# A streaming Conformer layer on one core: the second block's first attention head gets the longer lag between its q and k request and its scores

## The chip, the cores and the metric

The kernel runs on one core of a Trainium2 chip. The metric is the device time of one execution in microseconds, as the median of several runs. A core has a matrix engine (TensorE, in the profile PE, its weight loads PEld), a vector engine (VectorE, DVE), a scalar engine (ScalarE, ACT), GpSimd (POOL) and SyncE (SP), whose queue issues most DMAs. Each engine works through its own instructions in order.

## The reference

One layer works on 2048 prompt rows and 64 sample rows of width 1024. A normalised and modulated input goes through one projection whose columns are a convolution pair, q, k, v and two gates; a causal depthwise convolution and a banded attention run on it, are gated, merged and projected; a feed-forward part follows.

```python
h = rms_norm(x, p['norm1_g']) * (1 + sc1) + sh1
z = h @ p['w_in']
glu_a, glu_b, q, k, v, g_conv, g_attn = jnp.split(z, offs, axis=-1)
u = glu_a * jax.nn.sigmoid(glu_b)
conv_out, conv_state = conv_module(u, conv_hist, ...)
q = rms_norm(q.reshape(B, T, N_HEADS, HEAD_DIM), p['q_norm_g'])
k = rms_norm(k.reshape(B, T, N_HEADS, HEAD_DIM), p['k_norm_g'])
o = attend(q, k, v, p['rel_bias']).reshape(B, T, ATTN_DIM)
attn_out = o @ p['w_attn_out']
merged = jax.nn.sigmoid(g_conv) * conv_out + jax.nn.sigmoid(g_attn) * attn_out
x = x + gt1 * (merged @ p['w_o'])
...
s = jnp.einsum('bqhd,bkhd->bhqk', q, k).astype(jnp.float32) * ATTN_SCALE
s = s + rel_bias[:, rel].astype(jnp.float32)[None]
p = jax.nn.softmax(jnp.where(mask[None, None], s, NEG_INF), axis=-1)
return jnp.einsum('bhqk,bkhd->bqhd', p, v)
```

There are 8 heads of 64 columns. Each frame reads its own chunk of 64 frames and the eight chunks before.

## The kernel before

All products in float32 are made of three matmuls on parts: `hh` and `hl` are the high and low part of the normalised input, `whi` and `wlo` those of a weight, and `mm3` issues hh·whi, hh·wlo and hl·whi into one accumulator `ps`. Three such matmuls are called a triple here.

The prompt and the sample are cut into four blocks of tokens (`PBLOCKS`; block 0 holds the 64 sample rows and 512 prompt rows, blocks 1 to 3 hold 512 each). `ORDER` runs for each block q, the first convolution stage, k, the second, v, the third and fourth, and the gates. In eight of the convolution stages of blocks 1 and 2 a step of the modulation is put in (`mod_steps`): products of `cl` with four slabs `wmod` of 512 KB into `pa`, and some microseconds later a short product with `sel` (`pa<-sel,R`). Four slabs are held; a slab's next load goes out when its products are done.

The attention of a block starts after its v (`heads`, `HEADS_NS`) and runs between the projection products of the stages that follow. It isn't written out in place. Each head is a generator (`attend`) in a lane, and a lane is pumped each time the emitted matmuls add up to `STEP_NS` of modelled PE time. The clock of all this is `stream.load["pe"]`, the planner's sum of modelled PE time in nanoseconds: a generator yields the time from which it may go on. PE's instructions stay in the order in which they were emitted (`manual_schedule` for PE); those of the other engines and of the DMA queues are ordered by a scheduler.

A head of block 1, 2 or 3 does this:

- `fetch` (L1491) requests q and k (`load_qk`, tiles `q2` and `kk`, one buffer each) and the bias, and sets in `loaded[i]` the planner time from which the scores may be emitted: `lag` after the request, `QK_LAG` = 9000 ns or `FIRST_LAG` = 14000 ns, and no less than `BIAS_LAG` = 6000 ns. For all but the first head of a block it is called when the last scores of the head before are emitted.
- four tiles of 128 queries: four matmuls `sc<-kk,q` of 320 columns each into `sc` (one buffer), then on DVE the row maximum with the bias added (`pr,sm<-sc,bias`, in the orders below an `ISA` row), the exponential on ACT, and the scaling on ACT.
- five groups of transposes (`ptp<-ident,pr`), the split into `ph` (ACT) and `pl` (DVE), and the products with v (`po<-ph,vv` and `po<-pl,vv`).

DVE also works through the 31 taps of the convolution (`y<-u,wd,y`), which the scheduler places around the row maxima; a tap is not to be issued ahead of the latest maximum emitted before it (`ahead_of_taps`).

`order` is the list of all heads as (block, head). In block 0 the prompt's heads (0, h) and the sample's ("s", h) alternate, so that the last one before (1, 0) is ("s", 7).

Of the kernel before, what the change touches and what calls it, by code (L numbers as in the profile page):

```python
# [622 lines left out]
def streaming_layer(ctx: ExitStack, tc: tile.TileContext, I, O):  # L623
# [845 lines left out]
    def load_bias(h):  # L1469
        for r in (0, HD):  # L1470
            nc.sync.dma_start(
                bias[r : r + HD, HD - r : 640 - r],
                bass.AP(tensor=rb_d.tensor, offset=rb_d.offset + 768 * h + HD, ap=[[1, HD], [1, 576]]),
            )
        return bias

    ahead_qk, spare = {}, {"open": False, "heads": []}
    order, loaded, now = [], {}, {"scored": -1, "finished": -1, "bias": None}
# [8 lines left out]
    def fetch_qk(i):  # L1487
        if i < len(order) and ("qk", i) not in now:
            x, h = order[i]
            if spare["open"]:  # L1490
                spare["heads"].append(i)  # L1491
            now["qk", i] = load_qk(x, h, *spans(x))

    def fetch(i):
        if i < len(order) and i not in loaded:
            x, h = order[i]
            fetch_qk(i)
            if now["bias"] is None or now["bias"][0] != h:
                now["bias"] = h, load_bias(h)
            first = x != "s" and (not i or order[i - 1][0] not in (x, "s"))  # L1500
            lag = FIRST_LAG if first else QK_LAG
            loaded[i] = max(stream.load["pe"] + BIAS_LAG, ahead_qk.get(i, stream.load["pe"] + lag))

# [5 lines left out]
    def attend(i):  # L1509
        x, h = order[i]  # L1510
        q0, nq, k0, nk = spans(x)
        yield lambda: now["scored"] == i - 1
        fetch(i)
        fetch_v(i)
        if not i:
# [7 lines left out]
        for t in range(0, nq, P):  # L1523
            n = min(P, nq - t)
            if x not in (0, "s"):
                ps = ps_a.tile([P, 2, 512], F32, tag="s", name="sc")
                for j in range(2):
                    for d in range(2):
                        pe.matmul(ps[:, j, :320], q2[:, d, t : t + P], kk[:, t + 320 * j : t + 320 * j + 320], start=d == 0, stop=d == 1)
                w, src, bs = 640, ps[:, :, :320], bias[:, ::-1]  # L1530
            else:
                w = nk if x == "s" else t + P

                if "banks" not in now:
                    sc = ps_a.tile([P, 2, 512], F32, tag="s", name="sc")
                    now["banks"] = [sc[:, 0:1], sc[:, 1:2]]
                ps = now["banks"].pop(0)
                now["banks"].append(ps)
                for d in range(2):
                    pe.matmul(ps[:n, 0, :w], q2[:, d, t : t + n], kk[:, :w], start=d == 0, stop=d == 1)  # L1540
                src, bs = ps[:n, 0:1, :w], bias[:n, 64:384][:, ::-1] if x == "s" else bias[:, :w][:, ::-1]
            pr, sm, free, ready = softmax_max(src, n, w, bs)
            tiles.append((pr, sm, n, w))
            if t + P < nq:
                yield free + PE_LAG, SCORE_ROOM
            else:
                fetch(i + 1)
                if (x, order[min(i + 2, len(order) - 1)][0]) in ((0, 0), ("s", "s")):
                    fetch_qk(i + 2)
                now["scored"] = i  # L1550
            if t:
                softmax_scale(*tiles[-2], x in ON_ACT)
# [827 lines left out]
```

## Time and profile before

| what | before |
|---|---|
| time, median of 3 runs | 2958.93 us (2955.85 to 2965.5) |
| time of the profiled execution | 2957.35 us |
| its span | 2955.5 us |
| instructions | 44837 |
| PE busy | 98% |
| DVE, ACT, POOL busy | 69%, 46%, 39% |
| DMA, mean over the span | 212 GB/s |
| granted PE clock, mean | 0.995 |

A busy time says how long an engine had instructions in flight. Idle time counts only where the engine that sets the end had it, which is PE here; its shares of the chain that ended last are 46% of the span in four lines of products alone. The span is that of the profiled execution; the runs that give the median are others. In rows of the timeline the first two numbers are the start and the duration in microseconds, `out<-in` are the tiles, and what stands in brackets is the idle time before and who ended it. Rows of one kind that follow each other closely are merged, and starts of merged rows can overlap.

### The profile page before, as it was taken

The numbers are of one execution on the slowest core, as the hardware profiler recorded it, in microseconds if no ns is written. First come the engines' busy times: TensorE is split into PE (matmuls) and PEld (weight loads), VectorE is DVE, ScalarE is ACT, GpSimd is POOL, SyncE is SP. The second block draws the span as 40 slices with busy tenths as digits, with TensorE's granted clock in tenths as the row PEclk, the third lists the DMA queues.
The fourth block names the chain that finished last, engine by engine and source line by source line (L and its number), as shares of the span: only waits on it lengthen the run. The fifth ranks groups of instructions, "written<-read, shape, count | busy, mean of one in ns | idle before, by whom it ended". The sixth has DMA issues, their size and how long they took to land.

```text
span 2955.5 us, 44837 instructions
## 1 busy us (share of the span) xinstructions
PE 2892.0 (98%) x16193; PEld 2586.7 (88%) x16193; DVE 2049.8 (69%) x3648; ACT 1364.3 (46%) x2453; POOL 1161.4 (39%) x753
## 2 busy tenths in 40 slices
PE   7999999999999999999999999999999999999999
PEld 5899777887888788888999998999999999999998
DVE  5897787668857885477777756666666547566666
ACT  3345533661465267464334345444444345444442
POOL 1101210111011102454666452366667742465767
PEclk9999999999999999999999999999999999999999
DMA  9989899878996897985444876232333965333333
GB/s 320 312 297 309 274 283 324 269 229 294 285 313 209 294 264 239 290 298 171 147 147 143 268 257 227 93 120 91 114 122 104 331 225 185 97 99 108 115 106 126
DMA packets 467067, 628.04 MB, mean 212 GB/s; under 512 B 36196, under 2 KB 314584, under 8 KB 466845
## 3 DMA queue, kind: packets, MB, share of 16 engines
q1 hardware_dynamic: 452944, 606.11, 63.4%
q10 hardware_dynamic: 13901, 19.08, 1.9%
q8 instruction: 127, 2.08, 0.3%
q14 instruction: 95, 0.78, 0.1%
HBM read 476.53 MB, written 148.54 MB: 211 GB/s over the span
## 4 chain that ended last, share of the span: by engine, by line
PE 46%; DVE 2%; DMA 2%; ACT 1%; issue 1%; POOL 1%; SPq 0%; ACTq 0%; DVEq 0%; POOLq 0%
PE ps L105 28%; PE pd L105 13%; PE pw L105 5%; DVE wlo L105 1%; DMA cin<-o_d 1%; ACT whi L105 1%; POOL wlo L105 0%; DMA tg<-g_d 0%; DVE ps L105 0%; ACT xn L105 0%; DMA wst<-in_w_ffn_in 0%; DMA wfo<-in_w_ffn_out 0%; DVE acc L105 0%; DVE sums L105 0%; PE pt L105 0%
## 5 line engine op out<-in xcount | busy, mean ns | idle before, releaser
L105 PE MATMUL ps<-t,whi 128*128 128x384 f32 (+1 forms) x2112 | 501.9, 322 | 3.2 <-DVE u L105 1.1
L105 POOL TENSOR_TENSOR wlo<-wst,whi 128x1024 fp32r<-128x1024 f32 (+1 forms) x159 | 362.7, 2293 | 233.7 <-ACT whi L105 195.6
L105 ACT ACTIVATE whi<-wst 128x1024 fp32r<-128x1024 f32 (+1 forms) x265 | 258.2, 979 | 316.5 <-PE ps L105 127.1
L105 PE MATMUL ps<-b,whi 128*128 128x384 f32 (+1 forms) x1584 | 380.6, 325 | 5.4 <-DVE v L105 2.1
L105 PEld LDWEIGHTS ps<-t,whi 128*128 128x128 f32 x2112 | 367.8, 188 | 10.6 <-ACT u L105 3.1
L105 DVE SCALAR_TENSOR_TENSOR y<-u,wd,y 128x512 f32<-128x512 f32 (+1 forms) x480 | 370.1, 773 | 7.5
L105 PE MATMUL ps<-hh,whi 128*128 128x512 f32 (+2 forms) x992 | 363.4, 366 | 0.1
L105 DVE TENSOR_TENSOR acc<-acc,pd 128x512 f32<-128x512 f32 x482 | 322.3, 685 | 48.7 <-PE pd L105 46.0
L105 PE MATMUL ps<-hh,wlo 128*128 128x512 f32 (+2 forms) x992 | 345.6, 348 | 0.3 <-DVE wlo L105 0.3
L105 PE MATMUL ps<-hl,whi 128*128 128x512 f32 (+2 forms) x992 | 345.2, 348 | 0.0
L105 PE MATMUL ps<-t,wlo 128*128 128x384 f32 (+1 forms) x1056 | 338.2, 321 | 0.0
L105 PE MATMUL pd<-whi,hid 128*128 128x512 f32 x912 | 297.5, 391 | 0.3 <-DVE hid L105 0.3
L105 PEld LDWEIGHTS ps<-b,whi 128*128 128x128 f32 x1584 | 276.8, 188 | 13.6 <-DVE v L105 3.2
L105 ACT ACTIVATE pr<-pr,sm 128x640 f32<-128x640 f32 (+2 forms) x272 | 202.1, 749 | 153.9 <-DVE sm L105 150.9
L105 PE MATMUL ps<-b,wlo 128*128 128x384 f32 (+1 forms) x792 | 256.0, 323 | 0.0
L105 POOL TENSOR_TENSOR r<-t,mhalf 128x1 f32<-128x1 f32 (+2 forms) x68 | 82.4, 1219 | 414.8 <-DVE t L105 375.0
L105 PEld LDWEIGHTS ps<-hh,wlo 128*128 128x128 f32 x992 | 187.3, 189 | 23.3 <-DVE wlo L105 0.5
L105 DVE TENSOR_TENSOR wlo<-wst,whi 128x1024 fp32r<-128x1024 f32 (+1 forms) x106 | 135.7, 1284 | 99.2 <-ACT whi L105 98.2
L105 PEld LDWEIGHTS ps<-hh,whi 128*128 128x128 f32 x992 | 187.7, 189 | 18.0 <-issue 2.9
L105 PEld LDWEIGHTS pd<-whi,hid 128*128 128x128 f32 x912 | 171.1, 188 | 36.5 <-DVE acc L105 0.8
L105 PEld LDWEIGHTS ps<-hl,whi 128*128 128x128 f32 x992 | 188.1, 190 | 14.5 <-issue 1.7
L105 PEld LDWEIGHTS ps<-t,wlo 128*128 128x128 f32 x1056 | 198.0, 188 | 0.8
(233 smaller groups left out, 6299.1 us busy)
## 6 DMA issues: line engine op xcount, KB each, us to landing
whi<-w_din_h SPq DMA_DIRECT2D x72, 512.0 KB, 5.2
wlo<-w_din_l SPq DMA_DIRECT2D x72, 512.0 KB, 7.8
wst<-sum_d SPq DMA_DIRECT2D x131, 256.0 KB, 2.9
wfo<-in_w_ffn_out SPq DMA_DIRECT2D x64, 512.0 KB, 4.1
wmod<-in_w_ada SPq DMA_DIRECT2D x46, 512.0 KB, 9.1
sum_d<-ws SPq DMA_DIRECT2D x88, 256.0 KB, 2.2
wst<-in_w_ffn_in SPq DMA_DIRECT2D x85, 256.0 KB, 3.2
wst<-in_w_in SPq DMA_DIRECT2D x40, 512.0 KB, 7.2
```

Source lines behind the costliest of these rows:

```text
L105: self.last = f(*args, **kw)
```

## The change

One line in `fetch` decides which heads get `FIRST_LAG`:

```diff
@@ -1497,7 +1497,7 @@
             fetch_qk(i)
             if now["bias"] is None or now["bias"][0] != h:
                 now["bias"] = h, load_bias(h)
-            first = x != "s" and (not i or order[i - 1][0] not in (x, "s"))
+            first = not i or x not in ("s", 0, order[i - 1][0])
             lag = FIRST_LAG if first else QK_LAG
             loaded[i] = max(stream.load["pe"] + BIAS_LAG, ahead_qk.get(i, stream.load["pe"] + lag))
```

Before, a head got it when it was the very first, or when the head before it belonged to another prompt block. After, the very first head and every head of blocks 1 to 3 whose predecessor is of another kind get it. The two conditions differ for one head alone, (1, 0), whose predecessor is the sample's: its lag goes from 9000 to 14000 ns of planner time. All later heads of block 1 are emitted relative to the one before and move with it; nothing is added to or taken from the work.

On PE, before, the scores of the second block's first head (`kk_5187`) come one triple after the short product with `sel`, and their fourth tile after the next modulation step (`wmod_5252` and its followers). `kk_5422` is the second head.

```order
L105 MATMUL pa_5223<-sel_193,R_5240 128x128 x2
...
L105 MATMUL sc_5297<-kk_5187,q2_5186 128x320 x4
...
L105 MATMUL sc_5329<-kk_5187,q2_5186 128x320 x4
...
L105 MATMUL sc_5356<-kk_5187,q2_5186 128x320 x4
...
L105 MATMUL pa_5375<-wmod_5252,cl_192 32x256 x4
...
L105 MATMUL sc_5412<-kk_5187,q2_5186 128x320 x4
...
L105 MATMUL sc_5527<-kk_5422,q2_5421 128x320 x4
```

On PE now, at the same place (`kk_5448` is the second head here, `pa_5355` the next modulation step):

```order
L105 MATMUL pa_5223<-sel_193,R_5240 128x128 x2
...
L105 MATMUL sc_5337<-kk_5187,q2_5186 128x320 x4
...
L105 MATMUL pa_5355<-wmod_5252,cl_192 32x256 x4
...
L105 MATMUL sc_5390<-kk_5187,q2_5186 128x320 x4
...
L105 MATMUL sc_5410<-kk_5187,q2_5186 128x320 x4
...
L105 MATMUL pa_5355<-sel_193,R_5372 128x128 x2
...
L105 MATMUL sc_5438<-kk_5187,q2_5186 128x320 x4
...
L105 MATMUL sc_5557<-kk_5448,q2_5447 128x320 x4
```

Nine triples stand ahead of the first scores and no longer one, and three of the four tiles come after the modulation products, not one. The modulation products have ten triples between them and the `sel` product in both orders, but one group of scores and no longer three.

On DVE, before, from the fourth row maximum of the first head to the first transposed tile of it (`pl<-ptp,ph`):

```order
L105 ISA pr,sm<-sc,bias 128x640
L105 ISA sm 128x1
L105 SCALAR_TENSOR_TENSOR y<-u,wd,y 128x512 x2
L105 RECIPROCAL sm<-sm 128x1
L105 SCALAR_TENSOR_TENSOR y<-u,wd,y 128x512 x3
L105 TENSOR_TENSOR A_173<-pa,cols 128x2x2x2
L105 SCALAR_TENSOR_TENSOR y<-u,wd,y 128x512
L105 TENSOR_TENSOR A_173<-A_173,cols 128x2x2x2
L105 SCALAR_TENSOR_TENSOR y<-u,wd,y 128x512
L105 TENSOR_TENSOR pl<-ptp,ph 128x512
```

On DVE now, from the same maximum past the first `pl` to the first maximum of the second head:

```order
L105 ISA pr,sm<-sc,bias 128x640
L105 ISA sm 128x1
L105 SCALAR_TENSOR_TENSOR y<-u,wd,y 128x512
L105 RECIPROCAL sm<-sm 128x1
L105 SCALAR_TENSOR_TENSOR y<-u,wd,y 128x512 x2
L105 RECIPROCAL sm<-sm 128x1
L105 SCALAR_TENSOR_TENSOR y<-u,wd,y 128x512 x8
L105 TENSOR_TENSOR pl<-ptp,ph 128x512
L105 SCALAR_TENSOR_TENSOR y<-u,wd,y 128x512
L105 TENSOR_TENSOR pl<-ptp,ph 128x512 x2
L105 SCALAR_TENSOR_TENSOR y<-u,wd,y 128x512
L105 ISA pr,sm<-sc,bias 128x640
```

Between the maximum and the first `pl` there are eleven taps now and seven before, and thirteen up to the second head's first maximum, with three `pl` between.

On SP the loads of q, k and the bias keep their places right behind the four wmod loads; further on, the weights, the x rows and the v loads of the block change places with those of the heads.

## The prediction

> **What bounds the kernel now.** I read the page's busy times first, then who TensorE (PE) waited for in the second block's stretch, then the timelines of PE, of the DMA queue on SP and of VectorE (DVE) around the longest wait found there.
>
> ```profile
> PE 2892.0 (98%) x16193; PEld 2586.7 (88%) x16193; DVE 2049.8 (69%) x3648; ACT 1364.3 (46%) x2453; POOL 1161.4 (39%) x753
> ```
>
> PE is busy for 2892.0 of 2955.5 us: only 63.5 us of idle time can be won anywhere, and the change touches one stretch. The instruction orders of the two kernels are the same on PE up to the second block's first head and again from the third block's first convolution products on, that is, outside 466 to some 710 us of this trace. In a stretch around it PE waited for this:
>
> ```profile
> PE sc L105 <- DMA kk<-k_d: 4.6, 2, 4.3
> PE pa L105 <- DMA wmod<-in_w_ada: 1.3, 2, 0.7
> PE pt L105 <- DVE kn L105: 1.0, 1, 1.0
> PE sc L105 <- DVE sm L105: 0.8, 1, 0.8
> ```
>
> Columns: total, times, longest. That is 7.7 us, and 4.3 of them are one wait of a head's scores for its keys. The PE timeline says which head:
>
> ```profile
> 466.54 0.82 PE L105 MATMUL sc<-kk,q 128*128 128x320 f32 x4
> 467.20 0.40 PE L105 MATMUL ps<-hh,whi 128*128 128x512 f32 x1
> 469.93 0.74 PE L105 MATMUL sc<-kk,q 128*128 128x320 f32 x4
> ...
> 475.32 1.07 PE L105 MATMUL pa<-wmod,cl 128*32 128x256 f32 x16
> 476.98 0.64 PE L105 MATMUL pa<-wmod,cl 128*32 128x256 f32 x8 [0.59 <-DMA wmod<-in_w_ada]
> 478.35 0.64 PE L105 MATMUL pa<-wmod,cl 128*32 128x256 f32 x8 [0.73 <-DMA wmod<-in_w_ada]
> 478.92 0.50 PE L105 MATMUL ps<-hh,whi 128*128 128x512 f32 x1
> 479.72 0.75 PE L105 MATMUL sc<-kk,q 128*128 128x320 f32 x4
> ...
> 490.31 0.40 PE L105 MATMUL ps<-hh,wlo 128*128 128x512 f32 x1
> 495.00 1.40 PE L105 MATMUL sc<-kk,q 128*128 128x320 f32 x4 [4.29 <-DMA kk<-k_d]
> 496.21 0.63 PE L105 MATMUL ps<-hh,whi 128*128 128x512 f32 x1
> 498.31 0.40 PE L105 MATMUL ps<-hh,wlo 128*128 128x512 f32 x1
> ```
>
> The first head, the one whose lag grows, starts its scores at 466.54 without a wait; its fourth tile is at 479.72. The long wait at 495.00 belongs to the **second** head. So the longer lag removes no wait of its own head; what it can do is move the heads against the other traffic.
>
> The wait costs more than 4.29 us. PE would have been free at 490.31 + 0.23 = 490.54, so 4.46 us are lost up to 495.00, and then it runs slowly:
>
> ```profile
> 475.00:480.00 5.00, 3.68 (x39) 1.68 (x38) 4.54 (x10) 1.75 (x3) 0.66 (x1) 1.00 1.05 410
> 490.00:495.00 5.00, 0.71 (x4) 0.27 (x3) 2.52 (x4) 0.60 (x1) 1.41 (x2) 0.98 0.63 172
> 495.00:500.00 5.00, 5.00 (x19) 4.27 (x20) 1.87 (x4) 0.92 (x2) 0.00 (x0) 0.67 0.75 219
> ```
>
> (Stretch, its length, busy time of PE, its weight loads, DVE, ACT, POOL; then granted clock, DMA share, GB/s.) The granted clock is 0.67 in the 5 us after the wait. The scores take 1.21 us to 496.21 where the head before took 0.66 (466.54 to 467.20), and the five matmuls from 496.21 to 498.31 take 2.10 us where five take 1.14 at the rate of 467.20 to 469.93 (twelve in 2.73): 1.5 us more. The wait is worth about **6.0 us**.
>
> **Why the keys were late.** The buffers of q and k are single, so their loads go out when the head before has done its fourth tile. Here they run into the modulation weights:
>
> ```profile
> 477.00 0.38 SPq L249 DMA_DIRECT2D wmod<-in_w_ada  x1
> 479.78 0.37 SPq L249 DMA_DIRECT2D wmod<-in_w_ada  x1
> 481.06 0.60 SPq L1427 DMA_DIRECT2D q<-q_d  x1
> 482.30 0.47 SPq L1428 DMA_DIRECT2D kk<-k_d  x1
> 484.94 0.45 SPq L1428 DMA_DIRECT2D kk<-k_d  x1
> 486.35 8.81 SPq L1471 DMA_DIRECT2D bias<-rb_d  x2
> ```
>
> Four wmod loads of 512 KB leave from 477.00 to 479.78, as PE lets go of the slabs; the DMA share of 475 to 480 is 1.05. q and k follow 1.3 us behind. The landing times of k, for the first head, this second one, and the six later ones of the block:
>
> ```profile
> DMA to landing us min/median/max: 6.6/6.6/6.6
> DMA to landing us min/median/max: 10.8/10.8/10.8
> DMA to landing us min/median/max: 4.7/6.1/7.5
> ```
>
> Only the load behind the wmod slabs took 10.8 us.
>
> **The change part by part.** Work is neither added nor taken away; the sum is waits alone. All times below are this trace's clock.
>
> *wmod, a loss.* In the changed order the wmod products stand before the second tile of the first head and not before its fourth, with the same ten projection triples ahead: PE comes there two score groups earlier, 2 x 0.6 = 1.2 us, at some 474.1. The slabs were issued by earlier products that do not move, so the last still lands at 478.35 and PE leaves at 478.92 as before. **+1.2 us** (bounds: 0, should the slabs land that much earlier, to 1.2 plus a spell of half clock).
>
> *Half clock after wmod.* PE then idles about 2.9 us in pieces within 4.8. Whether that lowers the clock is bounded by two rows:
>
> ```profile
> 309.31 0.50 PE L105 MATMUL sc<-kk,q 128*128 128x256 f32 x2 [2.86 <-DVE sm L105]
> 310.00:315.00 5.00, 5.00 (x28) 5.00 (x27) 2.88 (x12) 4.44 (x11) 1.96 (x3) 0.66 0.96 334
> ```
>
> 2.86 us in one piece lowered it to 0.66 over the next 5 us; the 1.3 us in pieces at 475 to 480 left it at 1.00. The case lies between them: 0 or 1.5 us, and I take **+0.7**. The Trainium skill (TensorE: Matmul & The Clock Gate, "What's actually happening") says that the clock is halved after at least one idle window of some 3.4 us, counted by a free-running window. By that rule pieces with work between them would cost nothing, and the sum would be 0.7 better; the wait of 2.86 us above, shorter than such a window, disagrees with its letter.
>
> *The second head's keys, the gain.* From 478.92 the changed order has a triple and the second tile (479.72, as the fourth had it), two triples and the third tile (some 481.7), then three triples and the small pa product before the fourth: 484.85. q and k leave 1.34 us behind the start of that tile, as at 479.72 and 481.06, so from 486.2, and the second half of k at about 488.15 with the 0.65 us of one issue. That is 8.4 us behind the last wmod load and no longer 5.2. With 4.7 to 7.5 us k lands between 492.9 and 495.7; with the worst, 10.8, at 499.0. PE, with nearly the same work between the heads (13 triples and 3 groups of transposes against 11, 4 and a few short products; 10.85 us), is at the second head's scores at 495.7. So the wait is 0, at worst 3.3 us plus its half clock, 4.8. I take 0, since seven of the eight heads lie at 7.5 us or less: **-6.0 us**.
>
> *DVE, a loss.* In the changed order DVE has 13 convolution taps between the fourth row maximum of head one and the first of head two, and PE's next tile waits for that maximum, since scores have one buffer. The prices:
>
> ```profile
> 512.75 5.48 DVE L105 SCALAR_TENSOR_TENSOR y<-u,wd,y 128x512 f32<-128x512 f32 x7
> 518.15 1.88 DVE L105 TENSOR_TENSOR pl<-ptp,ph 128x512 fp32r<-128x512 f32 x3
> 519.95 0.82 DVE L105 CUSTOM_DVE_ANT_0 pr<-sc,bias 128x640 f32<-128x640 f32 x1
> 520.68 0.08 DVE L105 DVE_READ_ACCUMULATOR2_ANT sm<- 128x1 f32 x1
> ```
>
> A tap takes 5.40 / 7 = 0.77 us, a pl 0.60, a maximum 0.73. The fourth maximum starts near 486.3 (two maxima, taps between them, behind the third tile); 13 taps, 3 pl and the small ones make 12.8 us: the first maximum of head two starts near 499.1 and ends near 499.85, while PE wants its second tile at 499.3. Again 18 taps, 6 tensor operations, 4 maxima and the small ones, 20.9 us, bring DVE to head three's first maximum at 520.0, done 520.7; PE, 19.5 us of work behind 499.9, wants the next tile at 519.4. Waits of 0.55 and 1.3 us; with taps 2% shorter, as the whole piece from 498.09 to 519.95 ran, half of it: **+1.3 us** (bounds 0, and 6.4 should each of the eight tiles of two heads wait the 0.8 us that the only such row of the stretch has).
>
> *Later heads.* The gap from one head's last tile to the next one's first is some 10 us or more in both orders; the loads there took at most 7.5 us to land. The other waits of the first list (0.3, 0.8 and 1.0) I leave as they are; they may go or double: 0, with 2.1 either way.
>
> The sum is -6.0 + 1.2 + 0.7 + 1.3 = -2.8 us. The profiled execution, 2957.35 us (a span of 2955.5 and 1.85 around it), becomes 2954.5. It lies 1.6 below the median of the runs shown, 2958.93; on that scale the forecast is **2956 us**, 0.1% faster.
>
> **The rivals.** *The wait travels with the head* (slower). Loads always leave behind the previous head's fourth tile, so k is late again: for it speaks that the gap of 10.85 us does not grow; against it the row of 10.8 us, the only one above 7.5, which sat right behind wmod. It decides from a landing of 10.8 us on: wait 3.3 and half clock 1.5 return, then -2.8 + 4.8 = +2.0, 2961.
>
> *DVE becomes the bound of the two heads* (slower): the eight tiles wait 0.8 us each, 6.4 for my 1.3: +2.3, again 2961. For it speaks DVE's lack of slack above; against it that the bias wait goes with which DVE lost 5.5 us before its first maximum of head two:
>
> ```profile
> 498.09 0.82 DVE L105 CUSTOM_DVE_ANT_0 pr<-sc,bias 128x640 f32<-128x640 f32 x1 [5.53 <-DMA bias<-rb_d]
> ```
>
> *A later head meets the next loads*: one wait like the old one, +6.0, 2962; two would give 2968. Against it: no later landing above 7.5.
>
> *Everything falls away*: no half clock, no DVE wait, the 2.1 of small waits gone: -6.0 + 1.2 - 2.1 = -6.9, 2952.
>
> *Nothing happens*, because the first head never waited and the second one's wait was cover for DVE, which would now wait by as much: 2959.
>
> **How the numbers follow.** Forecast 0.52; wait travels 0.14; DVE 0.13; later head 0.08; everything falls away 0.08; nothing 0.05. The range runs from 2950 (the best case less some 2 us of scatter) to 2964 (the later head's wait and 2). All cases but two late heads lie within 8.9 us of the old median, which is 0.3%, about what a measurement of this kernel can tell from no change; the runs shown spread over 9.65 us themselves, so scatter of the medians gives a little to both sides: faster 0.08, same 0.85, slower 0.07.
>
> **What would show it.** Right: no wait for kk near 495 and a granted clock of 1.00 in 495 to 500; wmod waits of about 2.5 us in sum near 474 to 479; score waits for DVE of about 1 us at the second tiles of heads two and three. Wrong: a kk landing above 9 us behind the second head's issue, a clock of 0.66 after the wmod products, or a wait above 3 us that starts anywhere between 500 and 710.

## The result, and the profile after

| | before | after |
|---|---|---|
| time, median of 20 runs each | 2959.11 us (2954.56 to 2965.5) | 2952.45 us (2946.94 to 2959.03) |
| ratio after to before, 95% interval | | 0.9975 (0.9968 to 0.9982) |
| profiled execution, its span | 2957.35, 2955.5 us | 2952.32, 2950.5 us |
| granted PE clock, mean | 0.995 | 0.996 |
| instructions | 44837 | 44832 |

The changed kernel is faster by 0.25%, 5 to 9.5 us by the interval. The forecast of 2956.0 had the sign and the range right and the gain too small: -2.8 us on the profiled execution's scale, of a gain of some 7.

The list of PE's waits of the changed kernel from 455 to 720 us (total, times, longest) answers to the list of four lines before:

```profile
PE pa L105 <- DMA wmod<-in_w_ada: 2.0, 3, 0.7
PE sc L105 <- DVE sm L105: 0.4, 1, 0.4
```

The wait for k (4.6) and the one for kn (1.0) are gone, that for sm is halved, and that for wmod has grown from 1.3 to 2.0. On the PE timeline of the changed kernel the modulation products stand first, and then the second head's first two score tiles:

```profile
473.02 0.64 PE L105 MATMUL pa<-wmod,cl 128*32 128x256 f32 x8
474.27 0.64 PE L105 MATMUL pa<-wmod,cl 128*32 128x256 f32 x8 [0.61 <-DMA wmod<-in_w_ada]
475.63 0.64 PE L105 MATMUL pa<-wmod,cl 128*32 128x256 f32 x8 [0.72 <-DMA wmod<-in_w_ada]
476.95 0.64 PE L105 MATMUL pa<-wmod,cl 128*32 128x256 f32 x8 [0.69 <-DMA wmod<-in_w_ada]
...
494.23 0.74 PE L105 MATMUL sc<-kk,q 128*128 128x320 f32 x4
497.80 0.74 PE L105 MATMUL sc<-kk,q 128*128 128x320 f32 x4
```

Where the kernel before had 4.29 us of idle time and 1.40 us for four matmuls, here are none and 0.74. The clock (the third number from the end of a row of the windows; the columns are those of the prediction's) stays at 1.00 behind the modulation products and in the stretch that had 0.67:

```profile
475.00:480.00 5.00, 3.69 (x28) 2.49 (x29) 2.31 (x7) 0.85 (x2) 0.54 (x1) 1.00 1.05 416
480.00:485.00 5.00, 5.00 (x28) 4.36 (x28) 4.96 (x11) 2.66 (x5) 0.00 (x0) 1.00 1.03 385
495.00:500.00 5.00, 5.00 (x29) 4.21 (x28) 4.96 (x11) 1.96 (x4) 0.87 (x2) 1.00 0.82 237
```

On SP's queue the distance between reload and load has opened:

```profile
475.65 2.73 SPq L249 DMA_DIRECT2D wmod<-in_w_ada  x4
484.18 0.60 SPq L1427 DMA_DIRECT2D q<-q_d  x1
...
486.12 0.60 SPq L1428 DMA_DIRECT2D kk<-k_d  x1
486.83 3.62 SPq L1471 DMA_DIRECT2D bias<-rb_d  x2
494.38 0.37 SPq L1434 DMA_DIRECT2D vv<-v_d  x1
```

The four wmod loads are out at 478.38, and q follows 5.8 us later; before it was 0.9 (from 479.78 + 0.37 to 481.06). The view of the tile kk gives the landing time of this load, counted from the issue of the first of its two halves:

```profile
DMA to landing us min/median/max: 7.1/7.1/7.1
```

**A measure for the stretch.** The profiled executions differ by some microseconds in places that no edit here touches, so I compare them between two fixed points: the starts of the modulation products ahead of everything that is moved and of those behind it, in the timeline of PE. Before:

```profile
459.90 1.93 PE L105 MATMUL pa<-wmod,cl 128*32 128x256 f32 x32
...
745.28 1.93 PE L105 MATMUL pa<-wmod,cl 128*32 128x256 f32 x32
```

And after:

```profile
458.87 1.93 PE L105 MATMUL pa<-wmod,cl 128*32 128x256 f32 x32
...
736.80 1.93 PE L105 MATMUL pa<-wmod,cl 128*32 128x256 f32 x32
```

The stretch took 285.38 us and takes 277.93: 7.45 less, which is the whole gain of the medians (6.7) and of the ratio (0.0025 x 2959 = 7.4). The two spans differ by 5.0 only, so 2.4 us went the other way outside the stretch. Two executions of the kernel before differ by as much there: its second look, below, has a span 1.5 us shorter and a stretch 0.9 us longer.

### The profile page after: what moved, and what is told of

It is laid out like the page before. It is cut to its first block, busy times and chain, and to the rows that moved or that the text cites. A ratio compares the mean times of both kernels' runs of the same rounds, so it can differ in the third digit from the quotient of the medians.

```text
span 2950.5 us, 44832 instructions
## 1 busy us (share of the span) xinstructions
PE 2890.8 (98%) x16193; PEld 2585.3 (88%) x16193; DVE 2046.4 (69%) x3648; ACT 1363.3 (46%) x2453; POOL 1162.6 (39%) x753
## 4 chain that ended last, share of the span: by engine, by line
PE 46%; DVE 2%; DMA 1%; ACT 1%; issue 1%; POOL 0%; SPq 0%; ACTq 0%; DVEq 0%; POOLq 0%
PE ps L105 28%; PE pd L105 13%; PE pw L105 5%; DVE wlo L105 1%; ACT whi L105 0%; DVE ps L105 0%; DMA cin<-o_d 0%; DMA x<-x_d 0%; DMA wst<-in_w_conv_out 0%; POOL wlo L105 0%; DMA wfo<-in_w_ffn_out 0%; DVE acc L105 0%; DVE sums L105 0%; DVE pw L105 0%; DMA tg<-g_d 0%
## 5 line engine op out<-in xcount | busy, mean ns | idle before, releaser
L105 PEld LDWEIGHTS ps<-t,whi 128*128 128x128 f32 x2112 | 367.7, 188 | 10.5 <-ACT u L105 3.3
```

Of the source, the lines that this page charges most:

```text
L105: self.last = f(*args, **kw)
```

## The experiments

Theory A: the gain is the second head's wait for k, because its load no longer goes out right behind the reload. Its rival B: the gain comes from the first head's own later scores and from the order of the work that goes with them. C and D are told where they come up. In the tables the ratio is that to runs of the kernel before on the same chip, with its 95% interval, and the stretch is measured as above. Each table's runs come from a chip of their own, and the first two rows of the first table from the result, so the ratio is what compares them.

### Four runs that move one thing each

**The second head's lag instead of the first's.** The change is undone, and head (1, 1) gets the longer lag:

```diff
-            first = not i or x not in ("s", 0, order[i - 1][0])
-            lag = FIRST_LAG if first else QK_LAG
+            first = x != "s" and (not i or order[i - 1][0] not in (x, "s"))
+            lag = FIRST_LAG if first or order[i] == (1, 1) else QK_LAG
```

> The change is undone and the longer lag is given to the second head of the second block instead: its k and q still go out right behind the 2 MB reload of the modulation weights, only its scores come some 5 us later; the first head stays where it was. Theory A (the gain is the second head's wait for k, 4.3 us and the half clock behind it): k still takes 10 to 11 us from issue to landing, but the wait is at most 0.5 us, the four modulation slabs keep their 3.6 us, and the time is 2951 to 2954. Theory B (the gain comes from the first head's own later scores and from what moves with them): nothing of that is here, the time is 2957 to 2960. Theory C (the wait travels with the head): it shows again, at 3 us or more, before the second or the third head's scores.

**The load before the reload.** The kernel before, with the reload's four issues put off by 12 us of planner time, which brings them behind the second head's q, k, bias and v. PE's order is exactly that of the kernel before; on DVE and ACT the scheduler places a few rows differently.

```diff
 class Slabs:
     def done(self):
         self.given += 1
-        self.stream.at(self.stream.when("pe"), lambda n=self.given: self.free(n), True)
+        held = 12000.0 if 28 < self.given <= 32 else 0.0
+        self.stream.at(self.stream.when("pe") + held, lambda n=self.given: self.free(n), True)
```

> The change is undone, and TensorE's order is that of the kernel before; the reload of four modulation slabs (four issues of 512 KB) is held back until the second head's q, k, bias and v have been issued. Theory A (the load is late because it goes out behind the reload): k lands in 6 to 8 us instead of 10.8, there is at most 0.5 us of wait before the second head's scores, the clock stays at full there, and the time is 2951 to 2954. Theory B (the first head's later scores bring the gain): TensorE's order is as before, so 2957 to 2960.

**The reload before the load.** The changed kernel, with three of the four issues put directly ahead of k:

```diff
 class Slabs:
     def done(self):
         self.given += 1
+        if self.given in (29, 30, 31, 32):
+            return
...
 def load_qk(x, h, q0, nq, k0, nk):
         for d in range(2):
             nc.sync.dma_start(q2[HD * d : HD * d + HD, :, :nq].bitcast(F32), ...)
+            if (x, h, d) == (1, 1, 0):
+                M.free(32)
```

> The change stays in, and TensorE's order is that of the changed kernel; three of the four issues of the modulation reload are held back until the second head's first q issue, so that they go out directly ahead of its k. Theory A: k is issued about 2 us later and lands in 9 to 11 us instead of 7.1, so the wait before the second head's scores is back at 2.5 to 5 us with up to 1.5 us of half clock: 2955 to 2959. Theory B (order of TensorE's work): as the changed kernel, 2951 to 2954.

**A smaller step.** `lag = 11000.0` for head (1, 0):

> The change in a smaller step: the first head's lag is 11000 instead of 14000. Only its first three score tiles come later, by 3, 2 and 2 steps of three projection products; its fourth tile, the modulation slabs and all that follows on TensorE stand as in the kernel before, and the reload and the second head's load leave as before. Theory A: the second head still waits 4 to 5 us for k with the clock halved behind it, and the time is as before, 2957 to 2960. Theory B (the gain grows with the first head's lag): about two fifths of the gain, 2955 to 2957.

| run | median us | ratio (interval) | stretch us | k lands in | wait for k, second head |
|---|---|---|---|---|---|
| before | 2959.11 | 1 | 285.38 | 10.8 | 4.29 |
| after | 2952.45 | 0.9975 (0.9968 to 0.9982) | 277.93 | 7.1 | none |
| second head's lag | 2952.44 | 0.9974 (0.9964 to 0.9985) | 277.66 | 10.5 | none |
| load before reload | 2950.08 | 0.9968 (0.9955 to 0.9981) | 278.06 | not shown | none |
| reload before load | 2957.40 | 0.9991 (0.9982 to 1.0000) | 283.83 | 7.8 | 2.37 |
| lag 11000 | 2961.07 | 1.0003 (0.9994 to 1.0012) | 292.13 | 10.9 | 4.62 |

All four went with theory A, and B falls: with PE's order of before and an early load the whole gain is there, and with PE's order of the change and a load right behind the reload most of it is lost (0.9991, whose interval reaches to 1). Of the 5.9 us that the stretch of this last run is longer than the changed kernel's, 1.2 come from two waits far behind this load, at 716 to 719 us (0.97 for `R`, 0.23 for a weight). The first run shows that an early load isn't needed: k took 10.5 us to land, hidden by the later scores. Theory C, that the wait travels to the next head, found nothing in it. On PE's timeline of the reload put first, the wait and the slow matmuls are back:

```profile
501.25 1.34 PE L105 MATMUL sc<-kk,q 128*128 128x320 f32 x4 [2.37 <-DMA kk<-k_d]
```

Four sizes missed: k landed in 7.8 us there, not in 9 to 11, its wait is just below the 2.5 expected, and the medians of the load before the reload and of 11000 lie 1 us below and 1 us above their ranges. Most of k's delay with the reload put first is in its issue: it left 3.1 us behind the start of the first head's fourth tile (487.89 to 490.98) and not 1.4 (483.40 to 484.83), since SP's queue had the three reloads ahead of it, and took 0.7 us longer to land. And the run with 11000 has a second wait, at its third head:

```profile
495.74 1.40 PE L105 MATMUL sc<-kk,q 128*128 128x320 f32 x4 [4.62 <-DMA kk<-k_d]
...
523.78 1.41 PE L105 MATMUL sc<-kk,q 128*128 128x320 f32 x4 [3.80 <-DMA kk<-k_d]
```

The third head's load took 10.3 us to land. That execution was the slowest of eleven; the second wait and the half clock behind it (0.70 and 0.62 in the two stretches of 5 us from 520) account for nearly all of what the stretch of 292.13 has more than the kernel before.

### Larger and middle steps, a second look, and both remedies

The first head's lag at 12500 and at 19000 (one number in the code), the kernel before once more, and the change together with the held reload of the second run.

> The change in an intermediate step: the first head's lag is 12500. From the last modulation product to the second head's first scores TensorE has 14.5 us of work, against 11.2 in the kernel before and 16.4 in the changed one, while the load still goes out a few us behind the reload. Theory A (what counts is when k lands against when its scores come): a wait of 1 to 2.5 us is left before the second head's scores, and the time lies between the two kernels, 2953.5 to 2957. Theory B, in its form that is left (the whole lag of the first head must be reached), gives 2957 to 2960.

> The change in a larger step: the first head's lag is 19000. The modulation products come before the first head's second score tile, and the second head's scores some 5 us later than in the changed kernel. Theory A: there is no wait left for k, so nothing more is gained: 2951 to 2954.5, no wait over 0.5 us before the second or the third head's scores. A rival of the prediction (VectorE, whose taps fill the longer gap, holds the second head's scores up): a wait of over 1 us for the maxima shows there, and 2955 or more.

> The kernel before once more, for a second profiled execution. If the third head's load stands at the edge in that kernel (it issues behind three loads of x rows and landed in 7.5 us without a wait in one execution, in 10.3 us with a wait of 3.8 us in the run with the lag of 11000), its landing lies between 7 and 11 us here and its wait between 0 and 4 us; if that one wait was an accident, there is none and the landing is about 7.5. The second head's wait is 4 to 5 us with the clock at 0.7 or less behind it in either case.

> The change, and the reload held back until the second head's q, k and bias have been issued. Both remedies take away the same wait, so by theory A they don't add: no wait for k, 2949 to 2953.5, which is within 2 us of the changed kernel. If the load's lateness cost something besides that wait (theory B, or a second reason), the time falls below 2948.

| run | median us | ratio (interval) | stretch us |
|---|---|---|---|
| lag 12500 | 2958.02 | 0.9998 (0.9988 to 1.0007) | 281.97 |
| lag 19000 | 2956.60 | 0.9995 (0.9985 to 1.0005) | 283.91 |
| before, second look | 2955.77 (one run) | | 286.25 |
| change and load first | 2952.65 | 0.9980 (0.9970 to 0.9990) | 279.22 |

In the second look the third head doesn't wait either (its k landed in 7.0 us, 7.5 in the first), so the 3.80 us above are no part of the kernel before. A third head waits again, for 2.00 us, in one run below; I take both for scatter between executions, which is not shown. The second head's wait is there in both looks, here a little above the 4 to 5 us expected:

```profile
496.37 1.40 PE L105 MATMUL sc<-kk,q 128*128 128x320 f32 x4 [5.25 <-DMA kk<-k_d]
```

Both remedies together gain no more than either alone, as theory A has it.

The other two missed, and they taught the most. With **12500** the wait for k is only 0.56 us, but nothing is gained. The timelines of its PE, of its DVE and of its SP queue, one after the other:

```profile
498.62 0.84 PE L105 MATMUL sc<-kk,q 128*128 128x320 f32 x4 [0.56 <-DMA kk<-k_d]
505.01 0.85 PE L105 MATMUL sc<-kk,q 128*128 128x320 f32 x4 [2.58 <-DVE sm L105]
```

```profile
504.13 0.82 DVE L105 CUSTOM_DVE_ANT_0 pr<-sc,bias 128x640 f32<-128x640 f32 x1 [5.20 <-DMA bias<-rb_d]
```

```profile
490.29 0.45 SPq L1428 DMA_DIRECT2D kk<-k_d  x1
498.85 1.09 SPq L1471 DMA_DIRECT2D bias<-rb_d  x2
```

PE waits for a row maximum, DVE waits with that maximum for the bias, and the bias was issued 8.1 us late. So there is a second late load. SP's waits name what held it, in the kernel before as well; first before, then after, from 480 to 500 us:

```profile
SPq L1471 <- DMA g_d<-gate: 7.9, 1, 7.9
```

```profile
SPq L1434 <- DMA g_d<-gate: 3.9, 1, 3.9
```

L1471 is the bias, L1434 is v, and `g_d<-gate` is a store of the gates that ACT's queue sends. Neither load needs its data. The compiled programs show the tie: the transfers of SP and ACT signal their completion on eight semaphores in turn, DMAHW0 to 7, and a transfer, unless something else already guarantees it, waits until the one eight places ahead has landed, which used the same semaphore. From the first wmod load of the reload on, other waits left out:

```
before                                  after
wmod   DMAHW6                           wmod   DMAHW6
wmod   DMAHW7                           wmod   DMAHW7
       (0: the gate store, on ACT)      wmod   DMAHW0
wmod   DMAHW1                           wmod   DMAHW1
wmod   DMAHW2                                  (2: the gate store, on ACT)
q      DMAHW3                           q      DMAHW3
kk     DMAHW4                           kk     DMAHW4
q      DMAHW5                                  (5: the next gate store)
kk     DMAHW6                           q      DMAHW6
bias   DMAHW7                           kk     DMAHW7
bias   DMAHW0  <- waits for the gate    bias   DMAHW0
vv     DMAHW1                           bias   DMAHW1
                                        vv     DMAHW2  <- waits for the gate
```

Before, the second half of the bias comes round to the semaphore of the gate store, can't be issued until that has landed (the store was issued at 486.83, the half at 494.71, after 7.9 us of waiting), and holds all of SP. After, the place falls on v, which isn't wanted until the head's products with v. Theory D follows: **two** loads of the second head were late, k and the bias, the wait for k covered the one for the bias, and the gain takes both. The earlier runs fit. With the second head's lag the bias left only at 496.28, as late as before, and the later scores hid it as they hid k (DVE waited 0.89 us, PE not at all); with the load before the reload it left at 481.98.

With **19000** no load is late, and it is lost elsewhere. PE's timeline and its windows there:

```profile
474.45 0.64 PE L105 MATMUL pa<-wmod,cl 128*32 128x256 f32 x8 [1.53 <-DMA wmod<-in_w_ada]
475.71 0.64 PE L105 MATMUL pa<-wmod,cl 128*32 128x256 f32 x8 [0.62 <-DMA wmod<-in_w_ada]
```

```profile
475.00:480.00 5.00, 3.18 (x30) 1.02 (x26) 4.17 (x7) 0.00 (x0) 0.45 (x1) 0.73 1.05 404
480.00:485.00 5.00, 5.00 (x16) 4.14 (x15) 0.46 (x1) 0.00 (x0) 0.00 (x0) 0.58 1.03 394
```

PE reaches the modulation products still earlier, waits 3.4 us in sum for their slabs, and the clock falls to 0.58. This is the prediction's loss on wmod, with the half clock, grown from 0.9 us to what eats most of the gain. Further on, at 639 to 642 us, PE waits 1.4 us for row maxima, and at 713 us 0.8 us for `R`; the second head's scores wait for none.

### Each of the two late loads alone

The next three runs set one right without the other, and the last repeats the best kernel beside them. **k early, bias late**: the kernel before, the reload moved behind q and k but ahead of the bias.

```diff
         self.given += 1
+        if self.given in (29, 30, 31, 32):
+            return
...
             fetch_qk(i)
+            if order[i] == (1, 1):
+                M.free(32)
             if now["bias"] is None or now["bias"][0] != h:
```

> The kernel before with TensorE's order unchanged and the reload of four modulation slabs moved behind the second head's q and k but still ahead of its bias: k is early, the bias stays late. Theory D (two loads are late in the kernel before, k and the second half of the bias, which SP can issue only when a gate store has landed, and the wait for k covers the wait for the bias): k lands in under 8 us and the wait for k is at most 0.5 us, but VectorE waits for the bias until some 497 to 499 us, and TensorE's second tile of that head waits 3 us or more for VectorE: 2955 to 2960, little of the gain. Theory A alone (only k counts): 2949 to 2953.

**Bias early, k late**: the kernel before with one slab of the four held back behind v, which turns the rotation by one place and leaves 1.5 MB ahead of k.

```diff
-        self.stream.at(self.stream.when("pe"), lambda n=self.given: self.free(n), True)
+        self.stream.at(self.stream.when("pe") + (12000.0 if self.given in (32,) else 0.0), lambda n=self.given: self.free(n), True)
```

> The kernel before with TensorE's order unchanged and one of the four slabs of the reload issued behind the second head's v. With one transfer fewer ahead, the gate store's place in the rotation of completion semaphores falls on v and no longer on the bias: the bias is early, k goes out behind 1.5 MB and stays rather late. Theory D: VectorE's wait for the bias is under 1 us, k lands in 7.5 to 10 us, the wait for k is still 1.5 to 4 us with up to 1.5 us of half clock: 2953.5 to 2957.5, part of the gain. If the bias alone were the cause, 2949 to 2953.

**12500 with the rotation turned**: the same edit with `(31, 32)`, on the run with the lag of 12500.

> The run with the first head's lag of 12500, TensorE's order unchanged against it, and two of the four slabs of the reload issued behind the second head's v, so that the gate store's place in the rotation falls on v and no longer on the bias. Theory D: in that run the wait that was left (2.6 us of TensorE for VectorE, 5.2 us of VectorE for the bias) was the bias, so both are under 0.7 us here and the time is that of the changed kernel, 2950 to 2954. If that run was slow for TensorE's or VectorE's order, the time stays at 2956 to 2960.

**The second run again:**

> The run with q, k, bias and v ahead of the whole reload once more, beside these three on one chip, to see whether it beats the changed kernel too: by theory D both late loads are early and the modulation products stay where they were, which saves the 0.9 us that the change pays there: 2949 to 2953, up to 2 us below the changed kernel.

| run | median us | ratio (interval) | stretch us | k | bias |
|---|---|---|---|---|---|
| k early, bias late | 2960.86 | 0.9991 (0.9982 to 1.0001) | 283.24 | early | late |
| one slab held | 2958.07 | 0.9993 (0.9984 to 1.0001) | 285.91 | late | issued early |
| 12500, two slabs held | 2952.06 | 0.9970 (0.9960 to 0.9981) | 277.38 | early | early |
| load before reload, again | 2951.21 | 0.9968 (0.9956 to 0.9980) | 278.40 | early | early |

All four went as theory D has it, the second with a reservation. With k early and the bias late, the wait only changes its name; PE, DVE and SP of that run:

```profile
489.30 0.75 PE L105 MATMUL sc<-kk,q 128*128 128x320 f32 x4
496.03 0.98 PE L105 MATMUL sc<-kk,q 128*128 128x320 f32 x4 [2.99 <-DVE sm L105]
```

```profile
495.05 0.82 DVE L105 CUSTOM_DVE_ANT_0 pr<-sc,bias 128x640 f32<-128x640 f32 x1 [1.35 <-DMA bias<-rb_d]
```

```profile
491.89 0.45 SPq L1473 DMA_DIRECT2D bias<-rb_d  x1
```

The second half of the bias was held for 6.1 us by the gate store, and the 5 us from 495 run at a clock of 0.66. DVE had its maximum 2 us earlier than I expected, hence a wait at the low end. The median lies just above the range, on a chip whose kernel before has 2960.83: by the ratio 0.0009 is gained, and the interval includes none. With one slab held, SP's wait for the gate falls on v as intended, and k is as late as ever (its second half took 10.6 us to land; its scores start 13.2 us behind its first issue at 481.11, against 12.7 in the kernel before):

```profile
494.29 0.83 PE L105 MATMUL sc<-kk,q 128*128 128x320 f32 x4 [3.63 <-DMA kk<-k_d]
```

DVE and SP of that run:

```profile
495.36 0.83 DVE L105 CUSTOM_DVE_ANT_0 pr<-sc,bias 128x640 f32<-128x640 f32 x1 [2.84 <-DMA bias<-rb_d]
```

```profile
484.95 2.45 SPq L1471 DMA_DIRECT2D bias<-rb_d  x2
```

Its 2958.07 lies just above what I expected, and its list puts 2.84 us of DVE's idle time down to the bias, where I expected less than 1; but that maximum starts at 495.36, 0.24 us behind the end of the scores that it also needs (494.29 + 0.83), so the bias cost no more than these 0.24 us. The reservation is that the bias was issued early but did not land early: it was out at 487.40, and DVE, which names it as the last thing it waited for, could start only 8 us later. Like k it lay behind the 1.5 MB. So an early issue of the bias alone is shown to gain little, but no run has k late and the bias landed early, and what k costs by itself is not measured. The third head of that execution waited 2.00 us for its k besides, so its stretch is no clean price of the second head's wait. And 12500 with the rotation turned is as fast as the change, with PE's and DVE's waits of the plain 12500 gone:

```profile
495.06 0.75 PE L105 MATMUL sc<-kk,q 128*128 128x320 f32 x4
498.63 0.74 PE L105 MATMUL sc<-kk,q 128*128 128x320 f32 x4
```

The two runs with the load before the reload, 2950.08 and 2951.21 us with a ratio of 0.9968 each, beat the kernel before clearly. Against the changed kernel's 0.9975 they are ahead by some 2 us, which the intervals don't separate.

## Why the prediction was right, and what it missed

**Half clock and wait of the second head, -6.0: right.** The runs of the two directions show both the wait and its cause, the reload ahead of the load. q left at 484.18, which is 485.2 on the clock of the trace before (the first fixed point stands at 458.87 and not at 459.90), where 486.2 was predicted, and k landed 7.1 us behind its issue, inside the 4.7 to 7.5 taken. The second look at the kernel before has 5.25 us in place of 4.29, and a granted clock of 0.52 and 0.79 in the two stretches of 5 us from 495; worked out in the same way, the term is 8.1 us there, an estimate, and some 7 in the mean of the two.

**wmod, +1.2: right, a little large.** From the first product to the end of the last it took 476.95 + 0.64 - 473.02 = 4.57 us, against 478.35 + 0.64 - 475.32 = 3.67 before: +0.9. The second look has 2.86 us here, so one execution each doesn't fix this term to better than a microsecond.

**Half clock behind wmod, +0.7: absent in the profiled execution.** The clock stayed at 1.00. It was a fair bracket all the same: the run with both remedies has the change's order on PE and the same three wmod waits (2.0 us in sum), and there the clock fell:

```profile
475.00:480.00 5.00, 2.92 (x35) 0.81 (x33) 3.54 (x8) 1.75 (x3) 0.66 (x1) 0.94 1.06 400
480.00:485.00 5.00, 5.00 (x26) 3.92 (x19) 2.23 (x5) 0.93 (x2) 0.00 (x0) 0.72 0.96 341
```

Its stretch is 1.3 us longer than the changed kernel's.

**DVE, +1.3: mis-sized; it measured 0.** DVE's timeline of the changed kernel from the first head's fourth maximum to the second head's first:

```profile
484.31 0.82 DVE L105 CUSTOM_DVE_ANT_0 pr<-sc,bias 128x640 f32<-128x640 f32 x1
...
487.18 5.37 DVE L105 SCALAR_TENSOR_TENSOR y<-u,wd,y 128x512 f32<-128x512 f32 x8
...
495.72 0.81 DVE L105 CUSTOM_DVE_ANT_0 pr<-sc,bias 128x640 f32<-128x640 f32 x1
```

The distance is 11.4 us where the step had 12.8, and on the clock of the trace before it began at 485.3 where the step had 486.3. The eight taps took 492.46 - 487.18 = 5.28 us, 0.66 each, against the 0.77 that the step took from seven taps before (the next operation starts at 492.46). In the compiled program these eight alternate between two rows of `y`, so that a tap waits for the one two places ahead, while the seven are one row, each waiting for the tap just ahead. I read the difference as that; it was not tested by itself. DVE was on time: PE's second tile (497.80) has no wait.

**Later small waits, 0: mis-sized; about -1.7.** The 1.0 for kn and the 0.3 for a later head's k are gone, and 0.8 for sm has become 0.4. The step had named 2.1 either way and taken the middle. With these sizes the sum is -6.0 + 0.9 - 1.7 = -6.8, against -7.45 measured over the stretch; the remaining 0.65 I can't assign. That is the prediction's rival "everything falls away" (2952), which had 0.08.

**The step that was not there.** The prediction let DVE's wait for the bias go without asking why the bias was late; it stood behind k's wait and looked like a part of it. The late half of the bias had a cause of its own besides the reload that it shared with k, and the rival that "the second one's wait was cover for DVE, which would now wait by as much" was the right description of it: by the ratios, k early with a late bias is worth 0.0009 of the 0.0032 that both bring, with an interval that includes none, and the lag of 12500 nothing that could be measured. The change escaped because the gate store came to stand two transfers later among the reload's and the load's, and a second one between the two halves of q and k, so that the rotation put v where the bias had been. The forecast had the right sign with one of its two conditions unseen; that the change met the other one too was luck, since the prediction nowhere asks when the bias leaves.

## What to carry to other kernels

A wait that ends last can cover a second one behind it: before pricing its removal, ask of every operand of the next few instructions when its own load was issued and what that issue waited for. Where a load waits on SP for a transfer that it has nothing to do with, look for what the two share (here a completion semaphore eight transfers on); moving any transfer across it shifts the wait to another load, and the gain can hang on which. To move the large reload behind the small urgent loads did the same as the change without touching PE's order, and a longer lag is no knob that only helps: 11000, 12500, 14000 and 19000 gave nothing, nothing, 0.25% and nothing clear of noise. And a load that is issued early has not landed early: with one slab held the bias went out 8 us sooner and was still only just in time for scores that were late themselves.

## What the runs showed of the hardware

The clock fell after shorter idle times than I had expected, and not always after the same ones. 2.37 us before the scores (the reload put first) were followed by 0.66 over 500 to 505 us, 2.58 us (the lag of 12500) by 0.66 over 505 to 510; 2.00 us (the third head, one slab held) by 1.00; and three pieces of 2.0 us in sum with products between them left 1.00 in the changed kernel and gave 0.72 with the load held first. The Trainium skill (TensorE: Matmul & The Clock Gate, "What's actually happening") has a window of some 3.4 us, free-running, that must be idle. The length agrees with these traces: the clock records from which the granted clock of a stretch is averaged hold only full and half, and in all fourteen traces the clock changes on a grid of 3.41 us (in the kernel before it is half from 494.85 to 498.26, in its second look for two such pieces). That the window must be idle throughout does not agree. With PE's idle time cut up by this grid, every piece of 3.41 us between 440 and 760 us that began at full clock and held 1.84 us or more of idle time was followed by half clock (2.37 with the reload put first, 2.46 with the lag of 12500, 1.89 with the load held first), and none with 1.63 or less was (1.63 in the changed kernel; the 2.00 us of the third head fall into two pieces, 1.43 and 0.58). So where a wait falls on the grid counts besides its length. Elsewhere in the traces pieces with 1.1 to 1.9 us of idle time went either way, so this border is not the whole rule.

The amount ahead of a load does not set its landing time alone: k took 10.8 us behind 2 MB, 10.6 behind 1.5 MB (one slab held) and 7.8 behind 1.5 MB (the reload put first). The view gives the time of one half of a load, which is the first half here except with one slab held, where it is the second.
